# A decoder trunk on one core: the projections of p moved to the end of the first input projections

## The chip, the core and the metric

The kernel runs on one core of a Trainium2 chip. A core has TensorE (matrix products into PSUM banks), VectorE and ScalarE (elementwise work; only they, not GpSimd, move data out of PSUM here), GpSimd (called POOL, which here clears small tiles and issues transfers) and SyncE (SP, which issues the weight transfers). Sixteen DMA engines move data between memory and the on-chip buffers. The metric is the time of one execution in microseconds, the median over several runs.

## The reference

Sequence length 1024, width 1024, two layers, batch 1, float32. For each layer:

```
y = RMSNorm(x) @ W_in + b_in      # split into mLSTM, HGRN2 and attention groups
x = x + concat(mLSTM(y), HGRN2(y), SWA(y)) @ W_out
x = x + relu(RMSNorm(x) @ W_up)^2 @ W_down                      # 1024 -> 4096 -> 1024
gate = sigmoid(RMSNorm(x) @ W_g)
x = x + gate * RMSNorm(p[l] @ W_p)                              # p: 1024 x 256, W_p: 256 x 1024
```

The last product, p[l] @ W_p, depends on inputs alone: on no x and on no earlier layer.

## The kernel before

The sequence is cut into two blocks of 512 rows, so that (l, b) names layer l and block b. Every large product runs through `gemm` (L372 to L400): four row tiles of 128 use four PSUM banks, and the contraction goes in slabs of 256. For each slab the weights come by one SP transfer into one of three `raw` buffers and are split into a high and a low part, `whi` on ScalarE (L364) and `wlo` on VectorE (L365); then 24 matmuls of 512 columns run, three for each of four row tiles and two halves of the slab (high by high, high by low, low by high). On the last slab an `evac` function takes each bank out. One slab is called a dense step here, and the generator yields after each. Lines L394 and L396 are the matmuls, L456 the transposes of a norm (`norm_T`), L346 and L347, or L349 and L350 with a scale, the split of an activation.

A pair (l, b) goes through these stages: norm and input projection (`IN_norm`, `IN`: six gemms of four dense steps, named skv, h, hig, sq, u, mvo), the mixers, `OUT_T` (L615 transposes) and `OUT` (two gemms of four steps), `MLP` (66 steps with the norm's two) and `PLE`, the gate phase: two steps of norm, two of the projection of p, eight of the gate. A projection loads p (L718, by POOL), transposes it (L724), splits it and runs two gemms of one dense step, 24 matmuls each; its evacuation copies a bank to a slot (L737) and sums its squares on ScalarE (L738). The gate's evacuation scales that result E (L761), forms the sigmoid and adds to x.

The mixers are generators, too: attention (`SWA`, 9 steps), HGRN2 (`HGRN`, 14) and `MLSTM` (9), two halves of each block. They are small operations on VectorE and ScalarE with small matmuls between. `Emitter.run` walks through the dense steps and after each adds a rate to an accumulator; for every whole 1.0 it emits one mixer step. Mixers of (0,0) mix into its own projection and that of (0,1), all others into the projection and MLP of the other block, at 0.7 and 0.9. `Emitter.flush` emits what is left before `OUT_T`. A mixer may start when its projections are done: HGRN after hig, attention after sq, mLSTM after mvo. Memory is handed out as 60 common slots and 10 for mixers.

Tile's scheduler turns this order into the order of each engine, with the program's order as priority; `high_priority(AHEAD)` moves weight splits and norm transposes up by 40 instructions, and evacuations by 100. On the chip the order of each engine and queue is fixed.

Of the kernel before, what the change touches and what calls it, by code (L numbers as in the profile page):

```python
# [10 lines left out]
F32 = mybir.dt.float32  # L11
# [5 lines left out]
AF = mybir.ActivationFunctionType  # L17
# [4 lines left out]
P = 128  # L22
# [13 lines left out]
AHEAD = 40  # L36
AHEAD_E = 100

RATE_IN00 = 1.9
RATE_IN01 = 2.5  # L40
RATE_IN = 0.7
RATE_MLP = 0.9
RATE_PLE = 0.9
# [1 line left out]
ROOM = tuple(22 - 4 * max(0, (n + 2) // 4) + 2 for n in range(24)) + (8,)  # L45
# [109 lines left out]
class Trunk:  # L155
    def __init__(self, ctx, tc, io, dims):
        self.tc, self.nc, self.io = tc, tc.nc, io
        self.L, self.S, self.FF = dims
        self.NB = self.S // NT
        ec = ctx.enter_context  # L160
        self.cp = ec(tc.tile_pool(name="const", bufs=1))
        self.wp = ec(tc.tile_pool(name="wts", bufs=2))
        self.sm = ec(tc.tile_pool(name="small", bufs=2))
        self.pg = ec(tc.tile_pool(name="pg", bufs=4, space=PSUM))
        self.pm = ec(tc.tile_pool(name="pm", bufs=4, space=PSUM))
        self.dp = ec(tc.tile_pool(name="spill", bufs=1, space=bass.MemoryType.DRAM))
        self.S_ = Slots(self.cp, NSLOT, MSLOT)

        self.xs_dram = [[[self.dp.tile([P, 512], F32, name=f"xsp{b}_{t}_{h}") for h in range(2)] for t in range(4)] for b in range(self.NB)]
        self.stat = [None] * self.NB  # L170
        self.X = [None] * self.NB
        self.X[0] = self.load_x(0, self.x_in, True)
        self.constants()
# [259 lines left out]

    def add_stat(self, b, X, t, h):
        self.nc.scalar.activation(self.junk, X[t][h][:, :512], AF.Square, accum_out=self.stat[b][:, 2 * t + h:2 * t + h + 1])  # L435

# [8 lines left out]

    def norm_T(self, X, gcols, own=False, stat=None):

# [3 lines left out]
        for h in range(2):  # L451
            with self.tc.high_priority(AHEAD):
                for k4 in range(4):
                    ps = self.bank()
                    for t in range(4):
                        nc.tensor.transpose(ps[:, t * P:(t + 1) * P], X[t][h][:, k4 * P:(k4 + 1) * P], self.ident)  # L456
                    hi, lo = self.get(), self.get()
# [249 lines left out]
            self.drop_T(T)  # L707
        yield from down(ng - 1)

    def PLE(self, l, b, last, between=None):  # L710
        nc, io, cols = self.nc, self.io, self.cols[l]
        X = self.X[b]
        pp = io["p"][l]

        src = [self.get() for _ in range(2)]
        for j in range(2):
            r0 = b * NT + j * 256
            nc.gpsimd.dma_start(src[j][:, :512].rearrange("p (t c) -> p t c", c=256), pp[r0:r0 + 256, :].rearrange("(t p) c -> p t c", p=P))  # L718
        Tp = []
        for k in range(2):  # L720
            ps = self.bank()
            for t in range(4):
                c = (t % 2) * 256 + k * P
                nc.tensor.transpose(ps[:, t * P:(t + 1) * P], src[t // 2][:, c:c + P], self.ident)  # L724
            hi, lo = self.get(), self.get()
            self.split(hi[:, :512], lo[:, :512], ps)
            Tp.append((hi, lo))
        self.put(*src)
        T = yield from self.norm_T(X, cols[:, C_PLE:C_PLE + 8])
        rg = self.mean_sq(b)  # L730
        self.rsqrt(rg, 4)
        E = [[None, None] for _ in range(4)]
        ms = self.small([P, 8], "ems")
        for nh in range(2):
            def evac(i, ps):
                E[i][nh] = self.get()
                nc.vector.tensor_copy(E[i][nh][:, :512], ps)  # L737
                nc.scalar.activation(self.junk, E[i][nh][:, :512], AF.Square, accum_out=ms[:, 2 * i + nh:2 * i + nh + 1])  # L738

            yield from self.gemm(Tp, lambda kp: self.wrows(io["w_ple_proj"][l], kp * 256, nh * 512, 512), 512, evac, False)  # L740
        self.drop_T(Tp)
        mv = ms.rearrange("p (t h) -> p t h", h=2)
        rs = self.small([P, 4], "ers")
        nc.vector.tensor_tensor(rs, mv[:, :, 0], mv[:, :, 1], op=ALU.add)
        nc.vector.tensor_scalar(rs, rs, 1.0 / D, EPS, op0=ALU.mult, op1=ALU.add)
        self.rsqrt(rs, 4)
        row = [self.get() for _ in range(2)]
        for h in range(2):
            nc.gpsimd.dma_start(row[h][:, :512], io["rowP"][l:l + 1, h * 512:(h + 1) * 512].broadcast_to([P, 512]))
        if not last:  # L750
            self.new_stat(b)
        for nh in range(2):

            rows = last and b == self.NB - 1 and nh == 1

            def evac(i, ps, c0=0, n=512):
                x, e = X[i][nh], E[i][nh]
                ys, sa = (self.get(1 if last and b == self.NB - 1 else None) for _ in range(2))
                w = 256 if rows else n
                if c0 == 0:  # L760
                    nc.vector.scalar_tensor_tensor(e[:, :512], e[:, :512], rs[:, i:i + 1], row[nh][:, :512], op0=ALU.mult, op1=ALU.mult)  # L761
                for c in range(c0, c0 + n, w):
                    y, a = ys[:, c:c + w], sa[:, c:c + w]
                    nc.scalar.activation(a, ps[:, c:c + w], AF.Abs, scale=rg[:, i:i + 1])
                    nc.vector.tensor_scalar(y, ps[:, c:c + w], rg[:, i:i + 1], 0.0, op0=ALU.mult, op1=ALU.min)
                    nc.scalar.activation(a, a, AF.Exp, scale=-1.0)
                    nc.scalar.activation(a, a, AF.Ln, bias=1.0)
                for c in range(c0, c0 + n, w):
                    y, a, sl = ys[:, c:c + w], sa[:, c:c + w], slice(c, c + w)
                    nc.vector.tensor_tensor(y, y, a, op=ALU.subtract)  # L770
                    nc.scalar.activation(y, y, AF.Exp)
                    nc.vector.tensor_tensor(e[:, sl], e[:, sl], y, op=ALU.mult)
                    nc.vector.tensor_tensor(x[:, sl], x[:, sl], e[:, sl], op=ALU.add)
                    if last:
                        r, q = b * NT + i * P, nh * 512 + c
                        nc.sync.dma_start(io["out"][r:r + P, q:q + w], x[:, sl])
                self.put(ys, sa)
                if c0 + n == 512:
                    self.put(e)
                    if not last:  # L780
                        nc.gpsimd.dma_start(self.xs_dram[b][i][nh], x[:, :512])
                        self.add_stat(b, X, i, nh)

            def wsrc(kp):
                return self.wrows(io["w_ple_gate"][l], kp * 256, nh * 512, 512)

            if rows:
                yield from self.gemm_rows(T, wsrc, evac)
            else:
                yield from self.gemm(T, wsrc, 512, evac, False)  # L790
            if between is not None and nh == 0:
                between()
        self.put(*row)
        self.drop_T(T)
# [428 lines left out]
def chain(*gens):  # L1223
    for g in gens:
        yield from g


@with_exitstack
def trunk_kernel(ctx: ExitStack, tc: tile.TileContext, io, dims):
    k = Trunk(ctx, tc, io, dims)  # L1230
    L = k.L
    assert k.NB == 2
    st = {}
    for l in range(L):
        st[l, 0], st[l, 1] = {}, {}
    em = Emitter(k.S_, WIDTH)
    last = L - 1

    def IN(l, b, between=None):
        return k.IN(l, b, st[l, b], lambda kind: em.queue.extend(k.MIX(l, b, st[l, b], kind)), between)  # L1240

    def norm(l, b):
        return k.IN_norm(l, b, st[l, b])

    def OUT(l, b):
        if "own" not in st[l, b]:
            em.flush((l, b), 0)
            k.OUT_T(l, b, st[l, b])
        em.run(k.OUT(l, b, st[l, b]))

    def tail(l, b, then=None):
        def ready():
            em.flush(then)
            k.OUT_T(*then, st[then])

        em.run(k.MLP(l, b), RATE_MLP)
        em.run(k.PLE(l, b, l == last, ready if then else None), RATE_PLE)

    em.run(chain(norm(0, 0), IN(0, 0, norm(0, 1))), RATE_IN00)
    k.bounds()  # L1260
    em.run(IN(0, 1), RATE_IN01, ROOM, (0, 0))
    OUT(0, 0)
    for l in range(L):
        tail(l, 0, (l, 1))
        OUT(l, 1)
        if l == last:
            tail(l, 1)
            break
        em.run(chain(norm(l + 1, 0), IN(l + 1, 0)), RATE_IN)
        tail(l, 1, (l + 1, 0))  # L1270
        OUT(l + 1, 0)
        em.run(chain(norm(l + 1, 1), IN(l + 1, 1)), RATE_IN)
# [49 lines left out]
```

## Time and profile before

| | |
|---|---|
| median of 3 runs | 2705.81 us (2704.51 to 2706.89) |
| profiled execution, its own time | 2703.17 us |
| its span, first to last instruction | 2701.5 us |
| mean granted TensorE clock | 0.996 |
| busy: TensorE, VectorE, ScalarE, POOL | 99%, 66%, 52%, 2% |

The busy share of TensorE is of matmuls as the profiler models their ends, and they overlap; so a second measure is how many matmuls a stretch holds. The granted clock is 1.00 for the upper level and 0.50 for the lower one.

### The profile page before, as it was taken

The page shows a single profiled execution, that of the slowest core. Times are in us where ns is not written, and L with a number is a line of the kernel's source. Part 1 is how long each engine was busy: PE and PEld are TensorE (multiplying, and loading weights), DVE is VectorE, ACT ScalarE, POOL GpSimd, SP SyncE. Part 2 cuts the span into 40 slices and gives each one's busy share as a digit, 9 for nine tenths or more (in the row PEclk, how much of TensorE's full clock was granted, in tenths as well). Part 3 has the DMA queues.
Part 4 walks back from the last instruction along what each step waited for, and adds up shares of the span by engine and source line. Part 5 has one row for each costly group of instructions (what it writes and reads, how often), then busy time and mean ns, then how long its engine had stood idle before and what let it go on. Part 6 is the DMA issues. An engine that isn't in the chain of part 4 may idle for free.

```text
span 2701.5 us, 35241 instructions
## 1 busy us (share of the span) xinstructions
PE 2663.3 (99%) x12848; PEld 2141.9 (79%) x12848; DVE 1771.1 (66%) x3744; ACT 1401.9 (52%) x2923; POOL 61.6 (2%) x148
## 2 busy tenths in 40 slices
PE   8999999999999999999999999999999999999999
PEld 6877788887777888887777888888777787888887
DVE  5797856667768655776666754767677575443447
ACT  5456545546646643555644654454664464443336
POOL 2000000000000100000000010000000000000000
PEclk9999999999999999999999999999999999999999
DMA  5222232222222533222223253222222233332332
GB/s 181 84 52 59 61 119 86 85 80 79 71 92 81 151 103 88 79 79 78 79 77 104 86 151 105 79 86 86 71 78 88 92 133 102 95 94 97 104 102 78
DMA packets 131869, 249.57 MB, mean 92 GB/s; under 512 B 13744, under 2 KB 18992, under 8 KB 131696
## 3 DMA queue, kind: packets, MB, share of 16 engines
q1 hardware_dynamic: 123968, 224.56, 27.0%
q0 software_dynamic: 6720, 21.78, 2.5%
q8 instruction: 101, 1.65, 0.3%
q10 hardware_dynamic: 1008, 0.99, 0.1%
q14 instruction: 72, 0.59, 0.1%
HBM read 238.90 MB, written 8.39 MB: 92 GB/s over the span
## 4 chain that ended last, share of the span: by engine, by line
PE 94%; DVE 4%; ACT 1%; issue 0%; DMA 0%; ACTq 0%; DVEq 0%
PE gbank L396 51%; PE gbank L394 32%; PE mbank L456 2%; PE mbank L862 1%; PE mbank L1050 1%; PE mbank L929 1%; PE mbank L899 1%; PE gbank L426 1%; PE mbank L1179 1%; PE mbank L1186 1%; PE mbank L1072 0%; DVE wlo L365 0%; PE mbank L1048 0%; DVE slot L689 0%; PE mbank L1189 0%
## 5 line engine op out<-in xcount | busy, mean ns | idle before, releaser
L396 PE MATMUL gbank<-whi,slot 128*128 128x512 f32 (+1 forms) x4160 | 1307.5, 392 | 5.1 <-ACT slot L349 5.0
L364 ACT ACTIVATE whi<-raw 128x512 fp32r<-128x512 f32 (+1 forms) x840 | 517.6, 621 | 851.5 <-PE gbank L396 497.6
L365 DVE TENSOR_TENSOR wlo<-raw,whi 128x512 fp32r<-128x512 f32 (+1 forms) x840 | 565.7, 680 | 569.1 <-ACT whi L364 566.2
L396 PEld LDWEIGHTS gbank<-whi,slot 128*128 128x128 f32 x4160 | 772.3, 188 | 180.2 <-ACT slot L349 5.4
L394 PE MATMUL gbank<-slot,whi 128*128 128x512 f32 x2560 | 834.7, 400 | 2.5 <-DVE slot L566 2.4
L396 PE MATMUL gbank<-wlo,slot 128*128 128x512 f32 (+1 forms) x2080 | 810.5, 390 | 1.9 <-DVE wlo L365 1.9
L394 PEld LDWEIGHTS gbank<-slot,whi 128*128 128x128 f32 x2560 | 480.7, 188 | 120.7 <-issue 5.0
L394 PE MATMUL gbank<-slot,wlo 128*128 128x512 f32 x1280 | 510.4, 399 | 2.1 <-DVE wlo L365 2.1
L396 PEld LDWEIGHTS gbank<-wlo,slot 128*128 128x128 f32 x2080 | 391.6, 188 | 85.4 <-DVE wlo L365 2.9
L394 PEld LDWEIGHTS gbank<-slot,wlo 128*128 128x128 f32 x1280 | 241.4, 189 | 57.3 <-DVE wlo L365 3.4
L689 DVE SCALAR_TENSOR_TENSOR slot<-gbank,nrs,slot 128x512 f32<-128x512 f32 x256 | 191.6, 749 | 50.1 <-PE gbank L396 46.4
L347 DVE TENSOR_TENSOR slot<-slot 128x512 fp32r<-128x512 f32 x144 | 99.1, 690 | 87.5 <-ACT slot L346 86.8
L675 ACT ACTIVATE slot<-gbank 128x512 f32<-128x512 f32 x128 | 75.1, 586 | 33.8 <-PE gbank L394 33.6
L346 ACT ACTIVATE slot<-slot 128x512 fp32r<-128x512 f32 x144 | 89.8, 630 | 2.7
L350 DVE SCALAR_TENSOR_TENSOR slot<-mbank,cols,slot 128x512 fp32r<-128x512 f32 x112 | 79.3, 745 | 14.9 <-ACT slot L349 14.2
L676 ACT ACTIVATE slot<-slot 128x512 f32<-128x512 f32 x128 | 80.6, 630 | 2.5
L349 ACT ACTIVATE slot<-mbank,cols 128x512 fp32r<-128x512 f32 x112 | 72.7, 689 | 16.7 <-PE mbank L456 16.6
L435 ACT ACTIVATE junk<-slot 128x512 bf16<-128x512 f32 x96 | 60.2, 627 | 34.1 <-DVE slot L689 17.0
L909 ACT ACTIVATE slot<-slot,snm 128x256 f32<-128x256 f32 (+1 forms) x128 | 61.8, 486 | 29.4 <-DVE snm L906 29.4
L456 PE MATMUL mbank<-ident,slot 128*128 128x128 f32 x384 | 67.4, 284 | 7.9 <-DMA slot<-in_x_dram 4.0
L1025 ACT ACTIVATE slot<-slot 128x256 f32<-128x256 f32 x56 | 23.5, 420 | 72.6 <-DVE slot L1024 72.5
L456 PEld LDWEIGHTS mbank<-ident,slot 128*128 128x128 f32 x384 | 47.8, 146 | 16.8 <-DMA slot<-in_x_dram 4.9
(267 smaller groups left out, 2196.0 us busy)
## 6 DMA issues: line engine op xcount, KB each, us to landing
raw<-in_w_up_dram SPq DMA_DIRECT2D x128, 512.0 KB, 3.7
raw<-in_w_down_dram SPq DMA_DIRECT2D x128, 512.0 KB, 3.5
raw<-in_w_in_dram SPq DMA_DIRECT2D x80, 512.0 KB, 3.6
raw<-in_w_ple_gate_dram SPq DMA_DIRECT2D x32, 512.0 KB, 3.5
raw<-in_w_out_dram SPq DMA_DIRECT2D x16, 512.0 KB, 4.2
raw<-in_w_out_dram SPq DMA_DIRECT2D x32, 256.0 KB, 4.3
slot<-in_x_dram POOLq DMA_DIRECT2D x24, 256.0 KB, 5.0
raw<-in_w_in_dram SPq DMA_DIRECT2D x16, 256.0 KB, 2.8
```

Source lines behind the costliest of these rows:

```text
L346: first = nc.scalar.activation(r_(hi), src, AF.Copy)
L347: nc.vector.tensor_tensor(r_(lo), src, hi, op=ALU.subtract)
L349: first = nc.scalar.activation(r_(hi), src, AF.Copy, scale=scale)
L350: nc.vector.scalar_tensor_tensor(r_(lo), src, scale, hi, op0=ALU.mult, op1=ALU.subtract)
L364: nc.scalar.activation(hi[:, :n], raw[:, kk, :n], AF.Copy)
L365: nc.vector.tensor_tensor(lo[:, :n], raw[:, kk, :n], hi.bitcast(F32)[:, :n], op=ALU.subtract)
L394: nc.tensor.matmul(banks[i], wa[:, sl], ta, start=first, stop=last)
L396: nc.tensor.matmul(banks[i][:, :n], ta, wa[:, :n], start=first, stop=last)
L456: nc.tensor.transpose(ps[:, t * P:(t + 1) * P], X[t][h][:, k4 * P:(k4 + 1) * P], self.ident)
L675: nc.scalar.activation(u[:, :512], ps, AF.Relu)
L676: nc.scalar.activation(u[:, :512], u[:, :512], AF.Square)
L689: nc.vector.scalar_tensor_tensor(x, ps, r2[:, i:i + 1], x, op0=ALU.mult, op1=ALU.add)
```

## The change

The projections of p of all four pairs (l, b) become a generator of their own, `PROJ`, and run in a chain behind IN(0,1), before OUT(0,0). Their results, 8 tiles of 128 x 512 for each pair, go to memory by POOL transfers, and `PLE` loads them back; the sums of squares stay on the chip. The gate phase has ten steps instead of twelve. The two rates of the first projections fall from 1.9 to 1.5 and from 2.5 to 1.8.

```
-RATE_IN00 = 1.9
-RATE_IN01 = 2.5
+RATE_IN00 = 1.5
+RATE_IN01 = 1.8
...
+        self.es_dram = [[[[self.dp.tile([P, 512], F32, name=f"esp{l}_{b}_{t}_{h}") for h in range(2)] for t in range(4)] for b in range(self.NB)] for l in range(self.L)]
+        self.ems = {}
...
-    def PLE(self, l, b, last, between=None):
-        nc, io, cols = self.nc, self.io, self.cols[l]
-        X = self.X[b]
+    def PROJ(self, l, b):
+        nc, io = self.nc, self.io
         pp = io["p"][l]
         src = [self.get() for _ in range(2)]
...
         self.put(*src)
+        ms = self.ems[l, b] = self.cst([P, 8], f"ems{l}{b}")
+        for nh in range(2):
+            def evac(i, ps):
+                e = self.get()
+                nc.vector.tensor_copy(e[:, :512], ps)
+                nc.scalar.activation(self.junk, e[:, :512], AF.Square, accum_out=ms[:, 2 * i + nh:2 * i + nh + 1])
+                nc.gpsimd.dma_start(self.es_dram[l][b][i][nh], e[:, :512])
+                self.put(e)
+
+            yield from self.gemm(Tp, lambda kp: self.wrows(io["w_ple_proj"][l], kp * 256, nh * 512, 512), 512, evac, False)
+        self.drop_T(Tp)
+
+    def PLE(self, l, b, last, between=None):
+        nc, io, cols = self.nc, self.io, self.cols[l]
+        X = self.X[b]
         T = yield from self.norm_T(X, cols[:, C_PLE:C_PLE + 8])
         rg = self.mean_sq(b)
         self.rsqrt(rg, 4)
         E = [[None, None] for _ in range(4)]
-        ms = self.small([P, 8], "ems")
         for nh in range(2):
-            def evac(i, ps):
+            for i in range(4):
                 E[i][nh] = self.get()
-                nc.vector.tensor_copy(E[i][nh][:, :512], ps)
-                nc.scalar.activation(self.junk, E[i][nh][:, :512], AF.Square, accum_out=ms[:, 2 * i + nh:2 * i + nh + 1])
-
-            yield from self.gemm(Tp, lambda kp: self.wrows(io["w_ple_proj"][l], kp * 256, nh * 512, 512), 512, evac, False)
-        self.drop_T(Tp)
+                nc.gpsimd.dma_start(E[i][nh][:, :512], self.es_dram[l][b][i][nh])
+        ms = self.ems[l, b]
...
-    em.run(IN(0, 1), RATE_IN01, ROOM, (0, 0))
+    projs = [k.PROJ(l, b) for l in range(L) for b in range(k.NB)]
+    em.run(chain(IN(0, 1), *projs), RATE_IN01, ROOM, (0, 0))
     OUT(0, 0)
```

## Rows read from the trace of the kernel before

In the names, DVE is VectorE, ACT is ScalarE, PE is TensorE and PEld its weight load.

**Rows 1.** The page: the span, TensorE's row of part 1, the chain's engines.

```profile
...
span 2701.5 us, 35241 instructions
...
PE 2663.3 (99%) x12848; PEld 2141.9 (79%) x12848; DVE 1771.1 (66%) x3744; ACT 1401.9 (52%) x2923; POOL 61.6 (2%) x148
...
PE 94%; DVE 4%; ACT 1%; issue 0%; DMA 0%; ACTq 0%; DVEq 0%
...
```

**Rows 2.** Windows of 50 us: from:to, length, busy us of each engine, clock, DMA share, GB/s.

```profile
...
800.00:850.00 50.00, 47.89 (x243) 38.60 (x242) 42.06 (x84) 31.89 (x73) 1.18 (x3) 0.97 0.24 75
...
2250.00:2300.00 50.00, 50.00 (x233) 39.96 (x232) 22.23 (x36) 23.69 (x45) 0.00 (x0) 1.00 0.28 86
2300.00:2350.00 50.00, 50.00 (x217) 40.31 (x216) 22.09 (x33) 21.22 (x36) 0.00 (x0) 1.00 0.31 95
...
```

**Rows 3.** The same view cut at the stages.

```profile
...
95.00:173.00 78.00, 76.80 (x451) 61.94 (x450) 72.54 (x164) 46.85 (x113) 0.23 (x2) 1.00 0.19 51
173.00:300.00 127.00, 121.36 (x651) 93.61 (x651) 100.12 (x321) 72.30 (x189) 0.23 (x2) 0.97 0.24 67
300.00:345.00 45.00, 40.09 (x197) 30.93 (x196) 39.62 (x103) 28.68 (x62) 0.94 (x3) 0.96 0.17 48
...
95.00:361.00 266.00, 254.26 (x1367) 199.41 (x1366) 221.98 (x602) 152.62 (x371) 4.84 (x13) 0.98 0.25 71
1030.00:1545.00 515.00, 512.65 (x2503) 411.48 (x2502) 357.70 (x783) 275.86 (x581) 3.07 (x5) 1.00 0.27 83
...
```

**Rows 4.** TensorE's waits, 95 to 361 us: for whom, us in total, times, longest.

```profile
...
PE gbank L394 <- DVE slot L566: 2.4, 1, 2.4
PE mbank L1153 <- DVE G L1140: 2.1, 1, 2.1
PE gbank L394 <- DVE wlo L365: 2.1, 2, 1.7
...
```

**Rows 5.** Windows of 10 us.

```profile
...
300.00:310.00 10.00, 7.58 (x32) 5.56 (x30) 10.00 (x27) 8.88 (x20) 0.00 (x0) 1.00 0.00 0
...
350.00:360.00 10.00, 10.00 (x45) 8.07 (x44) 4.65 (x10) 1.59 (x3) 2.24 (x5) 1.00 0.90 256
...
```

**Rows 6.** Timeline, IN(0,1) to OUT(0,0): start, us, engine, line, instruction.

```profile
...
360.65 1.91 PE L615 MATMUL mbank<-ident,slot 128*128 128x128 f32 x16
...
361.39 2.41 ACT L349 ACTIVATE slot<-mbank,cols 128x512 fp32r<-128x512 f32 x4
...
362.32 0.47 PE L396 MATMUL gbank<-whi,slot 128*128 128x512 f32 x1
...
```

**Rows 7.** By line, 833 to 856 us (gate phase of (0,0)): count, busy us, mean ns.

```profile
...
L737 DVE COPY slot<-gbank 128x512 f32<-128x512 f32 x8 | 5.4, 687 | 1.3 <-PE gbank L396 1.3
...
L365 DVE TENSOR_TENSOR wlo<-raw,whi 128x512 fp32r<-128x512 f32 x4 | 2.7, 687 | 0.7 <-ACT whi L364 0.7
L738 ACT ACTIVATE junk<-slot 128x512 bf16<-128x512 f32 x8 | 5.0, 626 | 4.3 <-DVE slot L737 2.1 <-DVE rt L328 1.7 <-DVE nrs L329 0.5
...
```

**Rows 8.** Timeline, MLP(1,1) to its gate phase.

```profile
...
2634.63 0.71 PE L724 MATMUL mbank<-ident,slot 128*128 128x128 f32 x5
...
2636.43 0.50 PE L396 MATMUL gbank<-whi,slot 128*128 128x512 f32 x1
...
```

**Rows 9.** Timeline of VectorE, the last mixer of (0,1).

```profile
...
863.05 0.68 DVE L958 TENSOR_REDUCE mms<-slot 128x8 f32<-128x512 f32 x1
...
870.76 0.68 DVE L965 TENSOR_TENSOR slot<-slot 128x512 f32<-128x512 f32 x1
```

**Rows 10.** Timeline of POOL around the gate phase of (0,0); reloads of x (KB each, us to landing).

```profile
...
757.01 1.44 POOL L718 DMA_DIRECT2D slot<-in_p_dram  x2 [168.22 <-PE gbank L394]
...
858.58 0.33 POOL L1099 MEMSET cbd<- 128x260 f32 x1 [25.95 <-DVE cbd L1205]
...
slot<-xsp POOLq DMA_DIRECT2D x16, 256.0 KB, 5.7
```

**Rows 11.** Transfers of w_out: landing.

```profile
...
DMA to landing us min/median/max: 3.5/4.3/10.6
```

## The prediction, made before the changed kernel was run

> **What bounds the kernel.** I read the page first. TensorE is busy 2663.3 of 2701.5 us and carries 94% of the chain that ended last [rows 1]; so only two things can move the time: TensorE work added or removed, and stretches in which TensorE waits or runs at its lower clock. The change adds no matmul, so I looked for those stretches. In a pure MLP stretch 217 matmuls take 50 us, 0.230 us each [rows 2]; that is the rate against which I cost dense work. Then I cut the span at the stages [rows 3]. TensorE idles 11.7 us (266 - 254.3) between 95 and 361 us, where the mixers of (layer 0, block 0) run inside the first projections. Between 1030 and 1545 us the same 64 mixer steps of (1,0) cost it 2.35 us of idle, at clock 1.00. In the early stretch the clock also falls: 0.97 over 127 us and 0.96 over 45 us are 3.8 + 1.8 = 5.6 us lost if TensorE was at work. So the first projections hold at most 17.3 us of loss, of which some 15 is more than the mixers cost elsewhere.
>
> What causes it? The waits of that stretch [rows 4]: TensorE waits for VectorE, for an evacuation (L566) that has not freed its bank, for weight splits (L365: 2.1 us for one kind of gemm), and for the mLSTM's small operations (L1140 before L1153). At 300 to 310 us VectorE is busy 10.00 of 10 us and TensorE only 7.58 [rows 5]. That is a queue on VectorE: mixers are emitted faster than it can take them, and dense work stands behind them.
>
> **The change, part by part.**
>
> *Rates.* I counted steps by the code. A mixer set is 2 x (9 + 14 + 9) = 64 steps, the last of each mixer empty. In the first projection HGRN may start after 14 of its 28 dense steps; the other 14, at 1.9, take 26 mixer steps, and at 2.5 the remaining 38 go into the first 15 of the 24 steps of IN(0,1). That is 64 over 29 dense steps, 2.2 each, and nine steps at the end get none. After the change 14 x 1.5 = 21 and 24 x 1.8 = 43 steps: exactly 64, over 38 dense steps, 1.7 each, the last on the last step of IN(0,1). The eight projection steps get none by count; they are cover for what VectorE still has in its queue before OUT_T needs it. The gain by two bounds: set (1,0), mixed at 0.7 and then 0.9, loses 2.35 us, so a straight line from 2.2 (17.3 us) to 0.9 gives (2.2 - 1.7)/(2.2 - 0.9) x 15 = 6 us. The stretch 95 to 173 us, which mixes at 1.9, idles only 1.2 us in 78 at clock 1.00 [rows 3]; were everything like that, 266 us would lose 4.1, and 13 are gained. But that stretch is HGRN alone, which asks less of VectorE than attention, and the average load does not fall (below). I take -11, nearer to the row at 1.9, with 6 and 15 as ends.
>
> *The moved work.* Four projections are 4 x 48 matmuls and 4 x 8 transposes: 192 x 0.230 + 32 x 0.104 (16 transposes in 1.67 us, from 360.65 to 362.32 [rows 6]) = 47.5 us that leave the gate phases and enter before OUT(0,0). Sum 0. With each, VectorE takes 8 copies and 6 splits (four of weights, two of p), 14 x 0.687 = 9.6 us of the 11.9 that TensorE needs; ScalarE as many operations at 0.626, 8.8 us and the squares' readouts [rows 7]. Both stay below TensorE, so the eight steps run at TensorE's rate.
>
> *A new boundary between projections.* In the gate phase the p transposes are followed by the norm's transposes, which fill TensorE while ScalarE and VectorE split: from the first transpose (2634.63) to the first projection matmul (2636.43) are 1.80 us [rows 8]. Chained, nothing stands in between. At IN(0,1) to OUT(0,0) the first scaled copy ends at 361.39 + 0.60 = 361.99, 1.34 us after the first transpose, and 16 transposes just cover it [rows 6]. Eight cover 0.83. So 0.5 to 1.0 us is bare at each boundary: 4 x 0.7 = +2.8; the ends are 0, if leftover mixers fill it, and 4.
>
> *The gate phases.* What is late next there? norm_T is then followed at once by the gate matmuls, as OUT is by the MLP; the stretch that holds OUT(1,1) to MLP(1,1) shows TensorE at 50.00 of 50 [rows 2]. Cost 0; if that cover were gone, one copy and one split, about 1.5 us, four times.
>
> *The mLSTM's waits* in the gate phase (800 to 850 us: 47.89 busy, clock 0.97 [rows 2]) belong to the mixer, not to the projection, whose evacuation is what runs beside it. They stay: 0, with -3 and +2 as ends.
>
> *A shorter run-up to OUT_T.* The MLP takes floor(66 x 0.9) = 59 mixer steps of (0,1). The five left need six steps of the gate phase; before, two more followed ahead of the flush, now none. The last real mixer step is followed by one dense step (24 x 0.230 = 5.5 us) instead of three. Its output chain took from 863.05 to 871.4 us, 8.4 us [rows 9], and the transposes that need it ran at 878.46. So they may be 3 us late, more if evacuations go first; 22 us of gate matmuls of the second half can stand before them or behind them. I take +1; ends 0 and 6.
>
> *Spill and reload.* 32 stores and 32 loads of 256 KB through POOL's queue. A reload takes 5.7 us to land, the issue of two p loads 1.44 us, so eight take at most 5.8 + 5.7 = 11.5 us. They need slots; p's loads got theirs at 757.01, when the MLP's matmul of L394 released them, 76 us before their use [rows 10]. I cost the reload at 0: hidden by the last of the MLP and by 22 us of gate matmuls. The stores are read by nobody for 400 us. What they can do is fill the DMA: 8 weight slabs of 512 KB, 8 p loads and 32 stores are 14.7 MB in 47.5 us. From 350 to 360 us 256 GB/s were a share of 0.90, so 284 at the full; 14.7 MB would take 51.7 us [rows 5]. Stores may lag in free slots, and only weights stop TensorE; the longest landing of a w_out slab was 10.6 us, the median 4.3 [rows 11], against three raw buffers, two dense steps or 11 us, of lead. I take 0, and 4 us as the upper end.
>
> The Trainium skill, "DMA: Bandwidth & Descriptors", section Specifications, gives a limit of about 358 GB/s for one core's HBM traffic; by it, as an estimate, the 14.7 MB need 41 us and this term is zero. The row's 284 would put it at 4 us. No stretch here moves more than the rows say.
>
> **Sum:** -11 + 2.8 + 1 = -7.2 us. The profiled execution took 2703.17 us, so its like would take 2696.0; the median of the runs is 2705.81, 2.6 above it, and I forecast 2698.6, which is 0.27% faster.
>
> **Rivals.**
>
> *VectorE's queue merely moves (no measurable change).* From 95 to 361 us VectorE is 222.0 / 266 = 83% busy. With 38 us more work and 48 us more TensorE time, less 11, it is 260 / 303 = 86%. The average load doesn't fall; only the peaks do. If the waits follow the average, the gain is the straight line's 6 us or less, the boundaries take 4, OUT_T 1: about 2704.8. For it: the averages. Against: the waits sit where VectorE is at 95 to 100%, and the nine steps without mixers at the end of IN(0,1) are slack that the new rates use.
>
> *The reload stands behind a mixer's memset (no change, or a little slower).* Until 858.58 POOL waits 25.95 us for the mLSTM of (0,1) before it clears cbd [rows 10]. If the eight loads come behind that, the last lands at about 858.9 + 5.8 + 5.7 = 870; the first gate evacuation is then due at about 833 + 3.5 + 22 = 858, VectorE runs in order, and weight splits stand behind its wait: +12 in one gate phase. 2698.6 + 12 = 2710.6. Against: p's loads were placed 100 us ahead of it.
>
> *Weights late in the projection stretch (slower).* If stores and p loads go ahead of a slab, landing passes the 11 us of lead; from there on each of eight steps loses the rest. At 14 us: 8 x 3 = 24 us, 2698.6 + 24 = 2723. For it: the 10.6 us landing at a share of 0.90. Against: 4.3 us is the median, and p's loads can go ahead of the stretch, which leaves 12.6 MB, 44 us at 284 GB/s.
>
> *All the excess goes* and the boundaries are filled: -15 to -17, 2690.
>
> **How the numbers follow.** Forecast as summed (2693 to 2700): 0.45. All the excess goes: 0.12. The queue moves: 0.25. Reload late: 0.08. Weights late: 0.10. 0.2% is 5.4 us, about what a measurement can tell here: 2700.4 and 2711.2 are the borders. The forecast and the full gain are faster, less a tenth for forecasts just past the border; the moved queue and most of the late reload are same. Faster 0.53, same 0.33, slower 0.14. The range takes the full gain's near half, the forecast, the moved queue and the late reload: 2690 to 2710; the forecast's own is 2693 to 2701.
>
> **What would show it.** Right: between 95 us and the new start of OUT(0,0), TensorE idles under 6 us with clock 0.99 or more; no wait for L566 or L365 above 1 us; the projections' 47.5 us show 217 matmuls per 50 us with gaps of about 0.7 us before each L724's matmuls; every later stage keeps its length less 12 us. Wrong: VectorE at 10 of 10 us in the last third of IN(0,1) again; waits of the new L737's copies or of raw slabs in the projections; POOL's loads of E starting after the memset of cbd; TensorE idle before OUT_T of (0,1).

## The result, and the profile after

The changed kernel took 2729.36 us (median of 4 runs, 2728.8 to 2732.32) against 2706.35 for the kernel before on the same chip (4 runs, 2704.51 to 2707.07): a ratio of 1.0094, 95% interval 1.008 to 1.0107. It is slower by 23.0 us between these medians and by some 25 us by the ratio; 2698.6 was forecast, and the range, 2690 to 2710, does not hold the time. The profiled execution took 2728.84 us.

The page first: span, busy times, and the chain's engines, which answer to [rows 1].

```profile
span 2727.1 us, 35401 instructions
...
PE 2670.1 (98%) x12848; PEld 2143.9 (79%) x12848; DVE 1771.6 (65%) x3744; ACT 1400.4 (51%) x2923; POOL 95.7 (4%) x212
...
PE 91%; DVE 4%; ACT 2%; issue 1%; DMA 1%; POOL 0%; SPq 0%; POOLq 0%; ACTq 0%
```

TensorE does the same 12848 matmuls, busy for 6.8 us longer, in a span longer by 25.6. So 18.8 us are new idle time, and the rest is matmuls that took longer. POOL has 34 us more, the 64 spill transfers. DMA had 0% of the chain that ended last and has 1% now; TensorE's share fell from 94 to 91%.

Cut at the stages, by the last evacuation of each OUT on VectorE's timeline (us; "due" is 47.5 or 4 x 11.9 us for the moved matmuls, and nothing else):

| stretch | before | after | due | lost |
|---|---|---|---|---|
| start to end of IN(0,1) | 360.65 | 350.0 | 0 | -10.65 |
| to last evacuation of OUT(0,0) | 49.9 | 127.2 | +47.5 | +29.8 |
| to that of OUT(0,1), gate phase (0,0) in it | 540.7 | 532.7 | -11.9 | +3.9 |
| to that of OUT(1,0), gate phase (0,1) | 662.6 | 650.2 | -11.9 | -0.5 |
| to that of OUT(1,1), gate phase (1,0) | 662.9 | 654.7 | -11.9 | +3.7 |
| to the end, gate phase (1,1) | 424.8 | 412.3 | -11.9 | -0.6 |

The last column adds up to the 25.6 us of the two profiled spans. Two rows carry it: the first projections won what was forecast, and the stretch behind them lost almost three times as much. Windows of the changed kernel, with the columns of [rows 2]; the first answers to [rows 3], the others go through the chained projections.

```profile
95.00:345.00 250.00, 245.60 (x1333) 194.06 (x1332) 209.52 (x567) 143.70 (x347) 1.99 (x7) 1.00 0.24 68
345.00:366.00 21.00, 15.70 (x83) 12.06 (x82) 18.41 (x42) 15.05 (x39) 5.82 (x10) 1.00 0.35 126
366.00:376.00 10.00, 7.26 (x20) 5.39 (x21) 5.48 (x12) 3.86 (x8) 0.00 (x0) 0.50 0.42 158
376.00:390.00 14.00, 9.32 (x42) 7.13 (x40) 8.58 (x15) 7.88 (x20) 5.80 (x10) 0.99 0.67 238
390.00:396.00 6.00, 3.52 (x10) 2.64 (x11) 1.29 (x2) 1.08 (x2) 0.00 (x0) 0.50 0.15 60
396.00:410.00 14.00, 10.38 (x44) 8.04 (x42) 7.84 (x12) 7.87 (x20) 5.81 (x10) 0.98 0.57 203
410.00:414.00 4.00, 2.79 (x12) 2.42 (x12) 0.00 (x0) 0.00 (x0) 0.00 (x0) 0.57 0.76 199
```

Up to 345 us the clock is 1.00 where it was 0.97 and 0.96, and TensorE idles 4.4 us. From 345 to 414 us it idles 20.0 of 69 us (69 less the six busy times, 48.97), and the three windows at 0.50 to 0.57, 20 us, are the clock's lower level, 1.2 GHz. The DMA is not full: its share is 0.76 at most, in the last 4 us, and 0.15 to 0.42 in the other two slow windows. From 366 us on none of the engines listed is busy for more than 75% of a window, so something is waited for. TensorE's waits from 345 to 480 us:

```profile
PE mbank L726 <- DMA slot<-in_p_dram: 18.0, 6, 4.1
PE mbank L1200 <- DVE slot L1196: 1.2, 1, 1.2
PE gbank L399 <- ACT slot L349: 1.2, 4, 0.5
...
```

L726 are the transposes of p (L724 before). They wait for p, not for weights. Why is p late? POOL's timeline, the first projection's stores (L737) and the next one's loads of p (L720):

```profile
354.54 0.56 POOL L737 DMA_DIRECT2D esp<-slot  x1 [36.74 <-DVE slot L735]
...
362.72 0.54 POOL L737 DMA_DIRECT2D esp<-slot  x1 [0.74 <-DVE rt L331]
363.26 0.72 POOL L720 DMA_DIRECT2D slot<-in_p_dram  x1
363.99 0.57 POOL L737 DMA_DIRECT2D esp<-slot  x1
364.56 0.72 POOL L720 DMA_DIRECT2D slot<-in_p_dram  x1
377.06 1.14 POOL L737 DMA_DIRECT2D esp<-slot  x2 [11.78 <-DVE slot L735]
```

The loads need nothing but free slots, and their rows show no wait of their own. But they stand in POOL's order behind seven and eight stores, and each store waits for VectorE's copy (L735) of a projection's result. So p is asked for when the projection in front is all but done. TensorE's timeline shows the price:

```profile
362.44 0.40 PE L399 MATMUL gbank<-whi,slot 128*128 128x512 f32 x1
366.67 1.11 PE L726 MATMUL mbank<-ident,slot 128*128 128x128 f32 x4 [3.84 <-DMA slot<-in_p_dram]
369.60 1.11 PE L726 MATMUL mbank<-ident,slot 128*128 128x128 f32 x4 [1.81 <-DMA slot<-in_p_dram]
```

Behind the wait the clock is 0.50 for 10 us. The Trainium skill, "TensorE: Matmul & The Clock Gate", section HAM oscillation, has this pattern: waits for loads between short runs of matmuls let the clock fall, so that each run starts slow. The trace agrees in what follows the waits, at all three boundaries (0.50, 0.50 and 0.57); the runs of matmuls here, 11 to 14 us, are longer than the waits, while in the page's example they are shorter.

### The profile page after: what moved, and what is told of

It reads as the page before. It is cut to its first block, busy times and chain, and to the rows that moved or that the text cites. A ratio compares the mean times of both kernels' runs of the same rounds, so it can differ in the third digit from the quotient of the medians.

```text
span 2727.1 us, 35401 instructions
## 1 busy us (share of the span) xinstructions
PE 2670.1 (98%) x12848; PEld 2143.9 (79%) x12848; DVE 1771.6 (65%) x3744; ACT 1400.4 (51%) x2923; POOL 95.7 (4%) x212
## 4 chain that ended last, share of the span: by engine, by line
PE 91%; DVE 4%; ACT 2%; issue 1%; DMA 1%; POOL 0%; SPq 0%; POOLq 0%; ACTq 0%
PE gbank L399 48%; PE gbank L397 31%; PE mbank L459 2%; PE mbank L876 1%; PE mbank L1064 1%; PE mbank L943 1%; PE mbank L913 1%; PE gbank L429 1%; DVE wlo L368 1%; PE mbank L1200 1%; PE mbank L1086 1%; PE mbank L1193 0%; DMA slot<-in_p_dram 0%; POOL esp L737 0%; ACT whi L367 0%
## 5 line engine op out<-in xcount | busy, mean ns | idle before, releaser
L368 DVE TENSOR_TENSOR wlo<-raw,whi 128x512 fp32r<-128x512 f32 (+1 forms) x840 | 565.7, 679 | 559.6 <-ACT whi L367 556.6
L459 PE MATMUL mbank<-ident,slot 128*128 128x128 f32 x384 | 72.9, 285 | 8.2 <-DMA slot<-in_x_dram 8.2
L754 POOL DMA_DIRECT2D slot<-esp x32 | 17.0, 538 | 1375.9 <-PE gbank L397 1364.7
```

What stands on the lines that cost most here:

```text
L368: nc.vector.tensor_tensor(lo[:, :n], raw[:, kk, :n], hi.bitcast(F32)[:, :n], op=ALU.subtract)
```

## The experiments

Theory: the order of POOL's queue costs the 30 us. Rivals: the DMA is full; the gate phases or the rates do it. The first four kernels stood beside 2703.93 us for the kernel before.

**p one projection ahead.** The loads of the next pair are issued ahead of the stores of the current one:

```diff
+        ahead = self.p_load(*pairs[0])
+        for n, (l, b) in enumerate(pairs):
+            src = ahead
+            if n + 1 < len(pairs):
+                ahead = self.p_load(*pairs[n + 1])
+            yield from self.PROJ(l, b, src)
```

> The changed kernel with p loaded one projection ahead: the loads for the next pair are issued before the stores of the current one. If p's loads are late because they stand behind the stores in POOL's queue, the 18.0 us of waits for p and the clock drops that follow them (20.5 us at the lower level, some 10 us lost) go: 2729 - 28 + 2 for the bare boundaries, about 2703 (2699 to 2709). If the stores saturate the DMA engines instead, an earlier issue only lands later and at most a third is regained: above 2718. If the cost is the copy and split behind each chain boundary, nothing but the load latency goes: 2712 to 2722.

Measured: 2706.9 us, ratio 1.0006 (0.9996 to 1.0016): 22.5 us back by the medians, from one change of order. TensorE's waits from 345 to 480 us, then the windows there:

```profile
PE gbank L399 <- ACT slot L349: 3.7, 2, 2.1
PE mbank L1226 <- DVE slot L1221: 2.4, 2, 1.7
PE mbank L1211 <- DVE slot L1207: 1.2, 1, 1.2
PE gbank L399 <- ACT slot L352: 0.6, 1, 0.6
```

```profile
345.00:370.00 25.00, 20.92 (x119) 16.51 (x120) 22.32 (x51) 18.01 (x44) 5.81 (x10) 1.00 0.42 149
370.00:392.00 22.00, 20.41 (x92) 16.26 (x91) 17.82 (x32) 15.54 (x40) 9.48 (x17) 1.00 0.77 270
392.00:414.00 22.00, 21.25 (x103) 17.26 (x102) 17.51 (x27) 16.05 (x37) 9.23 (x18) 1.00 0.76 262
```

No wait for p, and the clock is 1.00 throughout. The same bytes now move at up to 270 GB/s, more than the 238 of the slow version: the DMA was not the limit. OUT(0,0) ends at 455.0 instead of 477.2 us.

**p loaded by SP.** `nc.gpsimd.dma_start` becomes `nc.sync.dma_start` for p.

> The changed kernel with p's loads issued by SP instead of POOL, in the same place of the program. If POOL's order is what makes them late, they are free of the stores now and the waits go as in the kernel with p loaded ahead, 2701 to 2712, with SP's weight transfers beside them as the only doubt. If the DMA engines are full, the queue makes no difference: 2722 or more.

Measured: 2715.81 us, ratio 1.0041 (1.0026 to 1.0056), between the two ranges; the waits for p are 5.7 us, three of them. SP's queue has an order too:

```profile
365.94 13.76 SPq L362 DMA_DIRECT2D raw<-in_w_ple_proj_dram  x3
379.79 0.97 SPq L720 DMA_DIRECT2D slot<-in_p_dram  x2
384.08 12.69 SPq L362 DMA_DIRECT2D raw<-in_w_out_dram  x2
396.86 0.97 SPq L720 DMA_DIRECT2D slot<-in_p_dram  x2
```

Both pairs of loads shown stand behind slabs that wait for a raw buffer: 13.76 us to issue three of them, 12.69 us to issue two. Another queue gives less than an earlier place in the same one.

**Each half of the change alone.** The new rates in the kernel before, and the moved projections with the old rates:

```diff
-RATE_IN00 = 1.9
-RATE_IN01 = 2.5
+RATE_IN00 = 1.5
+RATE_IN01 = 1.8
```

> The kernel before with the two new rates alone, the projections of p left in the gate phases. If IN(0,1) ends 10.7 us earlier because of the rates, that comes without the projections, too, and only the last mixer's output chain (some 8 us, less what the weights of OUT cover) is bare before OUT_T: 2696 to 2702. If the rates work only with the projections behind them as cover, the mixers' rest runs bare at the flush: 2704 to 2712.

> The changed kernel with the old rates 1.9 and 2.5: the move alone. If the rates gave the 10.7 us in IN(0,1), they are lost again, and p's loads are as late as before: 2736 to 2742. If the earlier end of IN(0,1) has another cause, the time stays at 2726 to 2732.

Measured: the rates alone 2702.21 us, ratio 0.9992 (0.9983 to 1.0002); the move alone 2738.68, ratio 1.0125 (1.011 to 1.014). So the rates are worth some 9 us beside the move (2738.68 - 2729.36 = 9.3; by the two ratios 8.4) and nothing that can be told without it. The time of the rates alone lies between its two ranges, so the trace has to say why they gain nothing. TensorE's timeline with the rates alone, then the window over it:

```profile
351.23 1.09 PE L615 MATMUL mbank<-ident,slot 128*128 128x128 f32 x8
...
361.26 1.12 PE L615 MATMUL mbank<-ident,slot 128*128 128x128 f32 x4 [8.03 <-DVE slot L965]
```

```profile
358.00:369.00 11.00, 7.02 (x19) 5.19 (x20) 10.74 (x22) 8.08 (x15) 0.00 (x0) 0.53 0.00 1
```

IN(0,1) ends 9.4 us earlier, and OUT_T then stands 8.03 us for the last mixer's output chain (L965, the 8.4 us of [rows 9]), with the clock at 0.53 behind it. The new rates need cover at their end; the moved projections are that cover, which the prediction named and did not price.

**Can milder rates do without cover?** The kernel before took 2703.3 us beside this one and the next three.

```diff
-RATE_IN00 = 1.9
-RATE_IN01 = 2.5
+RATE_IN00 = 1.6
+RATE_IN01 = 2.0
```

> The kernel before with rates between the two (1.6 and 2.0): the last three of the 24 dense steps of IN(0,1) get no mixer step, three times 5.5 us of cover for the output chain of the last mixer, which stood bare for 8.03 us in the run of the new rates alone. Theory (what the new rates lacked there was cover behind the last mixer): no wait of the OUT_T transposes for VectorE over 1 us, the gain of the earlier end stays, 2693 to 2699 us. Rival (the earlier end needs the new rates in full; at 2.0 attention stays too dense): 2701 us or more, with waits for VectorE and ScalarE of the kernel before in the last third of IN(0,1).

Measured: 2701.33 us, ratio 0.9993 (0.9984 to 1.0001), within the rival's range. OUT_T no longer waits, but the waits within the projections are back ("PE gbank L394 <- DVE slot L566", 4.4 us in one; clock 0.74 from 280 to 300 us), and OUT_T starts at 363.3 us, not earlier than the 360.65 of the kernel before.

**What is left with p ahead.** Mixers of the gate phase at 1.8 per dense step (`RATE_PLE = 1.8`); transposes and split of p also a projection ahead, between the two gemms of the one in front; and both:

```diff
                 yield from self.gemm(Tp, ...)
+                if nh == 0 and more:
+                    Tn = self.p_T(ahead)
```

> The kernel with p loaded a projection ahead (2706.9 us), and in addition the mixers of the gate phase at 1.8 per dense step, so that the set (0,1) ends after the third gate step, as it did in the kernel before. Theory A (the gate phase (0,0) loses its 3.9 us because the mixer's end moved nearer to OUT_T): the wait for ScalarE at the split of weights there goes, with the clock's 3.4 us, some 2703 us. Theory B (it loses them because the gate's evacuations now come right behind one another and the weight splits of OUT stand behind them): no change, 2705 to 2709 us. The gate phase (1,0) keeps its wait of 2.4 us in both.

> The kernel with p loaded a projection ahead (2706.9 us), and in addition p transposed and split a projection ahead, between the two halves of the projection in front. Theory (the boundaries cost what TensorE waits there for ScalarE's copy of p, 2.1 + 1.6 us and less): these waits go, some 2703 us. Rival (the waits are a queue of ScalarE that will stand elsewhere): no change, 2705 to 2709 us, with other waits for ScalarE in the projections.

> Both additions together. If each regains its part, some 2699 us; if one does, 2703; if neither, 2705 to 2709 us.

Measured: 2702.62 us, ratio 0.9997 (0.9988 to 1.0006), for the gate's rate; 2708.66, ratio 1.0021 (1.0012 to 1.003), for the split; 2705.68, ratio 1.0006 (0.9997 to 1.0014), for both, within the range expected if neither regained its part. The gate phase (0,0), TensorE's timeline and a window with p ahead alone, then windows with the gate's rate added:

```profile
919.88 1.21 PE L399 MATMUL gbank<-whi,slot 128*128 128x512 f32 x4 [2.11 <-ACT whi L367]
```

```profile
915.00:925.00 10.00, 7.49 (x27) 5.39 (x27) 8.84 (x20) 7.75 (x20) 1.63 (x3) 0.83 0.42 151
```

```profile
905.00:947.00 42.00, 42.00 (x190) 33.95 (x189) 38.36 (x67) 35.26 (x70) 5.91 (x11) 1.00 0.37 123
915.00:925.00 10.00, 10.00 (x53) 8.23 (x52) 9.90 (x17) 9.97 (x21) 1.41 (x3) 1.00 0.26 87
```

With mixers that end earlier the wait is gone, and the clock holds: OUT(0,0) to OUT(0,1) takes 530.3 us instead of 532.8. The cause was the shorter run-up to OUT_T, theory A; the total's intervals alone, 1.0006 and 0.9997, would not settle it. The split ahead gained nothing (its interval and that of p ahead alone overlap): the waits for ScalarE fell to 0.2 us, but it pulled the transposes half a projection nearer to the loads, and "PE mbank L728 <- DMA slot<-in_p_dram" came back with 5.1 us. That suggested loads two projections ahead (kernel before 2703.85 us, here and for the next two):

> All four moved, p split a projection ahead and mixers of the gate phase at 1.8, as in the run of both additions (2705.68 us), and p loaded two projections ahead of its use in place of one. Theory (the waits for p's load came back there since the transposes moved half a projection towards the load, which stands behind the stores): no wait for in_p_dram, 4 to 5 us less, 2700 to 2702 us. Rival (TensorE waits anyway, for VectorE's copies of the evacuations): 2704 us or more.

Measured: 2700.42 us, ratio 0.9986 (0.9978 to 0.9995). No wait for p is left. All four projections moved then cost nothing, but most of the rates' gain is still eaten: from 345 to 373 us TensorE idles 3.65 us, the clock is 0.76 in the first half of that, and the gate phase (1,0) keeps its wait of 2.4 us.

**One projection as cover.** Only one pair is moved; the other three are computed in their gate phases, as before (the edit is against the version with p ahead, and the lines that keep the other three in place are left out):

```diff
-    pairs = [(l, b) for l in range(L) for b in range(k.NB)]
+    pairs = [(1, 1)]
```

> The new rates, and only one projection moved behind IN(0,1): that of (1,1), whose gate phase has no mixer beside it; the other three are where the kernel before has them. Theory (the new rates gain some 10 us and lack only 8 us of cover behind the last mixer, which one projection's 11.9 us give; the rest of the move costs): 2703 - 10 + 1.3 for its one boundary, no loss in the gate phases, 2693 to 2697 us, no wait of OUT_T for VectorE over 1 us. Rival (the gain of the rates is only borrowed: what the mixers leave undone stands on VectorE and ScalarE ahead of OUT(0,0) also here): 2700 us or more, with waits or half clock between 345 and 425 us.

> As the run that moves (1,1) alone, with (0,0) moved in its stead, whose gate phase has the mixers of (0,1) beside it and their flush behind it. Theory (a gate phase that loses its projection loses 3 to 4 us where a flush follows it): 3 to 4 us more than the run that moves (1,1), some 2697 to 2700 us, with the wait for ScalarE's split of weights behind the gate phase (0,0). Rival (that loss comes of the projections' other effects, such as later weights): the same time as the run that moves (1,1).

Measured: 2689.96 us for (1,1), ratio 0.9947 (0.9934 to 0.9961); 2692.98 us for (0,0), ratio 0.9964 (0.9951 to 0.9976). Moving (1,1) is the fastest version found, faster than both kernels. OUT_T still waits 2.4 us for VectorE (L1008) in both, which the expectation had ruled out. TensorE's waits from 835 to 960 us, first with (1,1) moved, then with (0,0):

```profile
PE mbank L1196 <- DVE G L1183: 2.1, 1, 2.1
```

```profile
PE gbank L399 <- ACT whi L367: 2.1, 1, 2.1
PE gbank L399 <- DVE wlo L368: 0.4, 1, 0.4
```

The first wait is the mLSTM's; with (0,0) moved it falls before 835 us. The wait at the weight split comes only where the gate phase has lost its projection, and the times differ by 3.0 us, as expected; the two intervals overlap, but OUT(0,0) to OUT(0,1) alone takes 540.5 us with (1,1) moved and 531.5 + 11.9 = 543.4 with (0,0). But both were 4 to 5 us faster than worked out, and the stages showed a gain that was no part of the theory: MLP(0,0), which neither kernel changes, was shorter by 1.5 us, and OUT(0,1) to OUT(1,0) by 2.4 and 2.2 us.

**Where the weights lie.** In just these two kernels the constant of 32 bytes per partition that keeps the squares had put the weight buffers on a multiple of 64 bytes. So the kernel before with one unused constant, and the kernel with (1,1) moved with a wider one (kernel before: 2704.24 us):

```diff
+    pad = k.cst([P, 8], "pad")
+    k.nc.vector.memset(pad, 0.0)
```

```diff
-        ms = self.ems[l, b] = self.cst([P, 8], f"ems{l}{b}")
+        ms = self.ems[l, b] = self.cst([P, 16], f"ems{l}{b}")[:, :8]
```

> The kernel before, with the same instructions in the same order, and one constant of 32 bytes per partition more (cleared once, read by nobody), which puts the weight buffers (raw, whi, wlo) 32 bytes further: on a multiple of 64 bytes, as they are in the two runs that move one projection, and in no other kernel here. There MLP(0,0) took 417.2 and 417.3 us from the last evacuation of OUT(0,0) to its own last, and 418.2 to 418.9 us in all the others. Theory (the place of the weight buffers makes the matmul stream 0.3% faster, whatever the change does): MLP(0,0) in some 417.3 us and 2694 to 2698 us. Rival (the faster stream comes of something else in those two kernels): MLP(0,0) in 418.2 or more and 2701 to 2706 us.

> The kernel that moves the projection of (1,1) alone (2689.96 us), with its constant for the squares 64 bytes wide instead of 32, which puts the weight buffers back on an odd multiple of 32 bytes. Theory (8 of its 14 us come from the place of the buffers, some 5 from the rates with their cover): 2696 to 2700 us, still faster than before, MLP(0,0) in 418.2 us or more. Rival (all 14 us come from the rates and the cover): 2688 to 2692 us.

Measured: 2695.11 us, ratio 0.9967 (0.9955 to 0.9979), for the unused constant; 2696.33 us, ratio 0.9972 (0.996 to 0.9983), for (1,1) moved with the buffers put back. VectorE's timeline, the last evacuations of OUT(0,0) and of MLP(0,0), in the kernel before and then with the constant:

```profile
410.53 0.68 DVE L652 TENSOR_TENSOR slot<-gbank,slot 128x512 f32<-128x512 f32 x1
...
829.21 0.73 DVE L689 SCALAR_TENSOR_TENSOR slot<-gbank,nrs,slot 128x512 f32<-128x512 f32 x1
```

```profile
408.37 0.68 DVE L652 TENSOR_TENSOR slot<-gbank,slot 128x512 f32<-128x512 f32 x1
...
825.30 0.73 DVE L689 SCALAR_TENSOR_TENSOR slot<-gbank,nrs,slot 128x512 f32<-128x512 f32 x1
```

418.68 us became 416.93, by placement alone; with (1,1) moved, putting the buffers back made 417.20 into 418.41. TensorE's own stream is what changes: in 300 us of MLP(0,0) without idle time, at clock 1.00, it takes 1448 matmuls in the kernel before (460 to 760 us) and with the buffers put back (467.5 to 767.5), and 1453 with the constant (458 to 758) and with (1,1) moved (467 to 767). So of the 14 us of the fastest version the rates with their cover are 7.9 (2704.24 - 2696.33), and the rest, some 6 us, is where the buffers lie; in the kernel before the same shift is worth 9.1. The kernel before and the changed kernel both lie on an odd multiple of 32 bytes, so their comparison is not touched by it.

## Why the prediction was wrong, step by step

*Failed: spill and reload, "I take 0".* That step, and with it "so the eight steps run at TensorE's rate", is where the 2698.6 went wrong. It said "only weights stop TensorE" and, in a rival, "p's loads can go ahead of the stretch". It priced the stores as bytes, 14.7 MB at 284 GB/s, and looked at the order of POOL's queue only for the reload, behind the memset of cbd. (The rate was read too low as well, and stretches do move more than its rows say: the kernel before moves 329 GB/s from 910 to 920 us, at a share of 0.98.) The order that mattered was readable from the diff: PROJ loads p first and stores last, so in a chain the loads of one stand behind the stores of the other. The stretch lost 29.8 us; TensorE waited 18.0 us of it for p, and the clock's lower level behind these waits cost some 10; loading p a projection ahead gave 22.5 us back.

*Right in number, wrong in cause: the rival "Weights late", 2723 us.* Eight steps that each lose some 3 us came near the measured time by luck: TensorE's waits in the stretch name no weights, and DMA was not full. Its chance of 0.10 was on another mechanism.

*Rates, -11: right in size for IN(0,1).* It ended 10.65 us earlier, TensorE idles 4.4 us between 95 and 345 us, and neither L566 nor L365 (now L569 and L368) is waited for; so inside the projections the "queue merely moves" rival is refuted. With the rates alone, though, a wait did move, to OUT_T (8.03 us): what was missing is that this gain hangs on cover behind it. How it depends on the rates stays open, and the near hit is partly luck: at 1.6 and 2.0 IN(0,1) ended no earlier than at 1.9 and 2.5, which neither the straight line nor the row at 1.9 would give. With one projection as cover and the buffers on an odd multiple of 32 bytes the whole is worth 7.9 us; of what is missing, 2.35 us are a wait of OUT_T for the last mixer (L1008, at 368.46 us) that one projection does not cover.

*Boundaries, +2.8: close in the sum, not in its parts.* It was worked out as 0.7 us at each of four, from the time of one copy. With p ahead, two waits for ScalarE's split of p are left, 2.13 and 1.59 us, 3.7 in all, and one of 0.6 for OUT_T's copies. The first of them is a queue on ScalarE, which shows no idle time from 355.28 us to the copy at 365.93 us that ended it.

*Gate phases, 0, and the shorter run-up, +1: too low.* (0,0) lost 3.9 us and (1,0) 3.7. In (0,0) it is the run-up: the run with the gate's mixers at 1.8 regains 2.5 us, and the run with (1,1) moved, in which (0,0) keeps its projection, has no such wait. Its ends were 0 and 6, the value taken was too near the lower. In (1,0) TensorE waits 2.4 us for VectorE's weight split (L368) with p ahead as well, and not where (1,0) keeps its projection; it is the "cover gone" case, named at 1.5 us each. It was not tried by itself, so that cause is argued from the waits.

*Reload behind the memset of cbd: refuted.* The reload of E starts at 898.04 us, and the memset follows at 925.00:

```profile
898.04 4.25 POOL L754 DMA_DIRECT2D slot<-esp  x8 [0.43 <-issue]
...
925.00 0.32 POOL L1113 MEMSET cbd<- 128x260 f32 x1 [21.66 <-DVE cbd L1219]
```

*mLSTM, 0: right.* TensorE's 2.1 us wait for L1140 (now L1154) stayed.

With the measured sizes the prediction's own sum reads -10.65 + 29.8 + 3.9 - 0.5 + 3.7 - 0.6, which is the 25.6 us.

## What to carry to other kernels

Before a step with both loads and stores is chained, write down the order that each issuing queue will get, and look for a load that stands behind a store which waits for computed data: issue the next step's loads ahead of this step's stores. A stage that is made to end earlier needs dense work behind its last chain; one projection of 11.9 us did most of that (2.35 us stayed bare), and four cost back what it gave. And when stages that a change does not touch get shorter or longer with it, look at where the buffers lie before crediting the change.

## What the runs showed of the hardware

Weight buffers (raw, whi, wlo, and what lies behind them) 32 bytes further, on a multiple of 64, made the kernel before faster by 0.33% (0.21 to 0.45) with the same instructions and one memset more; the matmuls of a stretch without idle time came 0.35% faster (1453 instead of 1448 in 300 us). Which of the buffers matters was not tried. Waits for p of up to 4.1 us at the boundaries were followed by 4 to 10 us at a granted clock of 0.50 to 0.57, so that 20 us of idle time cost some 30; with waits for ScalarE of 2.13 and 1.59 us in their place the clock stayed at 1.00. Yet in the same run a wait of 2.11 us at a weight split, with one of 0.4 behind it, came with a clock of 0.83 over 10 us, so the length of a wait alone does not tell.
